# Stick-breaking attention: masks by GpSimd instead of matmuls, and softplus summed over later blocks before the sums' matmuls

## The chip, the cores and the metric

The kernel runs on one core of one Trainium2 chip. The metric is the device time of one execution in microseconds (us). Engines are named as in the profile: PE is TensorE's matmul side, PEld its weight load, DVE is VectorE, ACT is ScalarE, POOL is GpSimd, SP is SyncE, whose queue issues the DMAs.

## The reference

A two-layer decoder trunk over 512 tokens of width 1024: SwiGLU feed-forward, token mixer, feed-forward in each layer. The change is in the mixer of layer 1, stick-breaking attention with 16 heads of 64:

```python
z = jnp.einsum('bhqd,bhkd->bhqk', q_blk, kf) * (dh ** -0.5)
causal = key_pos[None, :] < q_pos[:, None]
log_stay = jnp.where(causal, jax.nn.log_sigmoid(-z), 0.0)
later = lax.cumsum(log_stay, axis=3, reverse=True) - log_stay
a = jnp.where(causal, jnp.exp(jax.nn.log_sigmoid(z) + later), 0.0)
return jnp.einsum('bhqk,bhkd->bhqd', a, vf)
```

With sp = softplus(z), the exponent is z minus the sum of sp over this key and all later ones that the query may see.

## The kernel before, in words

Every matmul operand is split in a high and a low fp32r half, so a product takes two or three matmuls. A head's scores stand with keys on partitions and queries on columns: for key block j (128 keys) only the queries from j*128 on, so the block has `size(j)` = 512 - 128*j columns. They are packed in three PSUM banks (tag `att`, four buffers): bank B holds blocks 1 and 3, bank C block 2, bank A block 0 (`PARTS`).

`stick_scores` (L758) is a head's first half. For each of the banks B, C, A it issues the score matmuls (L765, recorded at L108) and then, on each block's first 128 columns, a mask matmul that adds -1e30 where the key is not earlier than the query (L767, operands `cmask` and `idr`). Then ACT takes Abs, Exp and Ln (L770, L90), DVE forms softplus as max(z, 0) + ln(1 + exp(-|z|)) in an SBUF tile `t` (L773), and DVE splits it into the halves of `sps` (`split_v`: a cast L215, a subtraction L216).

`stick_weights` (L778) is the second half. For each block it adds, on top of z in PSUM, minus the sum of softplus over the block's own keys (`tri`, a triangle of -1) and over every later block (`nones`, a full matrix of -1), by the table `adds`: block 1 takes `nones` over blocks 3 and 2, block 0 over 3, 2 and 1, each in two halves. ACT then takes Exp into `w`, and `split_v` makes the two halves for `attend`, which multiplies with the values into `po`; ACT L529 copies a half of `po` and DVE L530 adds the two.

`stick` (L801) writes PE's order out by hand: with `order["on"]` every matmul depends on the one issued before it. `Flow` is a generator of projection steps of three 512-column (or six 256-column) matmuls each, which are put between the halves of a head: weights of head h, 2 steps, scores of head h+1, 5 steps, `attend` of head h, 5 steps. A finished projection of q or k is scaled by DVE (L547), split (ACT L476, DVE L477) and moved into place by DMAs (L482). The other engines' orders come from a scheduler, so they change with the program.

Tile slots: `t` 5 (both `t` and `w` use them), `sp` 3, `c2` 3 (bank C's halves), `misc` 1.

Of the kernel before, what the change touches and what calls it, by code (L numbers as in the profile page):

```python
# [16 lines left out]
F32R = mybir.dt.float32r  # L17
AF = mybir.ActivationFunctionType
ALU = mybir.AluOpType

P = 128
SEQ = 512
# [6 lines left out]
NEG = -1.0e30  # L29
# [5 lines left out]
def trunk(ctx: ExitStack, tc: tile.TileContext, a: dict, out: bass.AP):  # L35
    nc = tc.nc
    cpool = ctx.enter_context(tc.tile_pool(name="cpool", bufs=1))
# [19 lines left out]
    def T(shape=(P, SEQ), dt=F32, tag="t"):  # L57
        return tmp.tile(list(shape), dt, tag=tag, name=nm(tag), bufs=TMPS[tag])
# [30 lines left out]
    def func(o, i, f, **kw):  # L89
        r = nc.scalar.activation(out=o, in_=i, func=f, **kw)  # L90
        tc.add_manual_dep(r.ins, act["load"].name, nosync, reason="table set order")
        act["used"].append(r.ins)
        return r
# [13 lines left out]
    def mm(*args, **kw):  # L107
        return ordered(nc.tensor.matmul(*args, **kw))  # L108
# [10 lines left out]
    def const_r(name, cols, tag=None):  # L119
        t = cpool.tile([P, cols], F32R, tag=tag or name, name=name)  # L120
        raw = T((P, cols))
        nc.sync.dma_start(raw, a[name])
        nc.vector.tensor_copy(t, raw)
        return t
# [88 lines left out]
    def split_v(hi, lo, src):  # L213

        nc.vector.tensor_copy(out=hi, in_=src)  # L215
        nc.vector.tensor_tensor(out=lo, in0=src, in1=f32(hi), op=ALU.subtract)  # L216
# [246 lines left out]
    def hl(b, tag):  # L463

        return T((P, 2, 256), F32R, "c2") if b[0] == "C" else B((P, 2, SEQ), F32R, tag)
# [289 lines left out]
        return ss  # L755


    def stick_scores(e, q, k, cm, idr):  # L758
        zs, sps = {}, {}
        for b in heads(e):  # L760
            wd = WIDTH[b]
            z = zs[b] = ATT()
            for i, (_, j, at) in enumerate(PARTS[b]):
                scores(z[:, at:at + size(j)], q, k, e, slice(j * P, SEQ), slice(j * P, j * P + P), True,
                       first=i == 0, last=False)  # L765
            for i, (_, j, at) in enumerate(PARTS[b]):
                mm(z[:, at:at + P], idr, cm, start=False, stop=i == len(PARTS[b]) - 1, skip_group_check=True)  # L767
            zw = z[:, :wd]
            t = T()[:, :wd]
            nc.scalar.activation(out=t, in_=zw, func=AF.Abs)  # L770
            func(t, t, AF.Exp, scale=-1.0)
            func(t, t, AF.Ln, bias=one)
            nc.vector.scalar_tensor_tensor(out=t, in0=zw, scalar=0.0, in1=t, op0=ALU.max, op1=ALU.add)  # L773
            sps[b] = hl(b, "sp")
            split_v(sps[b][:, 0, :wd], sps[b][:, 1, :wd], t)
        return zs, sps

    def stick_weights(e, zs, sps, tri, nones):  # L778
        bb, bc, ba = heads(e)

        adds = {2: [(nones, bb, 3 * P, P), (tri, bc, 0, 2 * P)],
                3: [(tri, bb, 3 * P, P)],
                1: [(nones, bb, 3 * P, P), (nones, bc, 0, 2 * P), (tri, bb, 0, 3 * P)],
                0: [(nones, bb, 3 * P, P), (nones, bc, 0, 2 * P), (nones, bb, 0, 3 * P), (tri, ba, 0, SEQ)]}
        banks = {}
        for b in (bc, bb, ba):
            wd = WIDTH[b]
            z = zs[b]
            for _, j, at in PARTS[b]:
                n = size(j)  # L790
                for i, (st, sb, s0, m) in enumerate(adds[j]):
                    for c in range(2):
                        mm(z[:, at + n - m:at + n], st, sps[sb][:, c, s0:s0 + m], start=False,
                           stop=i == len(adds[j]) - 1 and c == 1, skip_group_check=True)
            w = T()[:, :wd]
            func(w, z[:, :wd], AF.Exp)
            banks[b] = hl(b, "ah")
            split_v(banks[b][:, 0, :wd], banks[b][:, 1, :wd], w)
        return banks

    def stick(ss, gcol_next):  # L801
        order["on"] = True
        q0, k0 = ACC(), ACC()
        proj_tile(("sb_q", 0), q0)
        r = norm_r(ss)
        proj_tile(("sb_k", 0), k0)
        rtm = token_r(r)
        r8 = T(tag="r2")
        nc.scalar.mul(out=r8, in_=r, mul=0.125)
        act_set(LNEXP)  # L810
        tri = const_r("tri", P, "bd")
        nones = const_r("nones", P)
        idr = cpool.tile([P, P], F32R, tag="idr", name="idr")
        nc.vector.tensor_copy(idr, ident)
        cm = const_r("cmask", P)
        outs, vs = [], [[] for _ in range(4)]
        q, k = [], []
        plain(q0, r8, lambda y: pack_q(y, "misc"), q)
        plain(k0, r, lambda y: pack_k(y, "misc"), k)

        def stream():
            yield from values(("sb_v", 0), rtm, vs[0])
            for i in range(1, 8):
                yield from plain_steps(("sb_q", i), r8, lambda y: pack_q(y, "misc"), q)
                yield from plain_steps(("sb_k", i), r, lambda y: pack_k(y, "misc"), k)
                if i in (2, 4, 6):
                    yield from values(("sb_v", i // 2), rtm, vs[i // 2])
            yield from out_first("sb_oa", outs)

        flow = Flow(stream())  # L830
        flow.run(16)
        z, o = None, None
        z = stick_scores(0, q[0], k[0], cm, idr)
        flow.run(12)
        for h in range(16):
            p, e = h // 2, h % 2
            banks = stick_weights(e, *z, tri, nones)
            flow.run(2)
            if h < 15:
                n = (h + 1) // 2  # L840
                flow.until(k, n + 1)
                z = stick_scores((h + 1) % 2, q[n], k[n], cm, idr)
            flow.run(5)
            flow.until(vs[p // 2], NB)
            if e == 0:
                o = T(tag="oo")
            attend(vs[p // 2], p, e, banks, o)
            if e == 1:
                out_pair(o, outs)
            flow.run(5)  # L850
        for _ in flow.steps:
            pass
        ss = out_second("sb_ob", outs, gcol_next)
        order["on"] = False
        return ss
# [13 lines left out]
    ident = cpool.tile([P, P], F32, tag="ident", name="ident")  # L869
# [39 lines left out]
def _constants():  # L909
    f = np.float32  # L910
    i = np.arange(P)
    c = {}
    c["ones_ms"] = np.full((P, P), 1.0 / D, f)
    c["bd"] = ((i[:, None] // DH == i[None, :] // DH) / DH).astype(f)
    c["ident"] = np.eye(P, dtype=f)
    c["tri"] = np.where(i[:, None] >= i[None, :], f(-1), f(0)).astype(f)
    c["nones"] = np.full((P, P), -1, f)
    c["cmask"] = np.where(i[:, None] < i[None, :], f(0), f(NEG)).astype(f)

    t = np.arange(SEQ, dtype=f)  # L920

    def angles(half, theta):
        inv = f(1.0) / (f(theta) ** (np.arange(half, dtype=f) / f(half)))
        return t[None, :] * inv[:, None].astype(f)

    ang = angles(32, 10000.0)
    cos, sin = np.cos(ang), np.sin(ang)
    rows_c, rows_s = np.zeros((P, SEQ), f), np.zeros((P, SEQ), f)
    for p in range(P):
        g, j = (p % DH) // 32, p % 32  # L930
        rows_c[p] = cos[g * 16 + j % 16]
        rows_s[p] = sin[g * 16 + j % 16] * (-1 if j < 16 else 1)
    lg = np.log1p(-(2.0 ** (-5.0 - np.arange(8))))
    for n, sign, scale in (("rot_q", 1, 1.0), ("rot_k", -1, DH ** -0.5)):
        dec = scale * np.exp(sign * lg[:, None] * np.arange(SEQ)[None, :])
        dec = np.repeat(dec.reshape(4, 2, SEQ), DH, 1)
        c[n] = np.concatenate([rows_c * dec, rows_s * dec], 2).astype(f)
    ang = angles(8, 500000.0)
    cos, sin = np.cos(ang), np.sin(ang)
    rows_c, rows_s = np.ones((P, SEQ), f), np.zeros((P, SEQ), f)  # L940
    for p in range(P):
        j = p % DH
        if j < 16:
            rows_c[p] = cos[j % 8]
            rows_s[p] = sin[j % 8] * (-1 if j < 8 else 1)
    c["rot_dil"] = np.concatenate([rows_c, rows_s], 1)

    dist = i[:, None] + (SEQ - P) - np.arange(SEQ)[None, :]
    mult = ((dist <= 128).astype(int) + (dist % 4 == 0) * (dist <= 512) + (dist % 16 == 0) * (dist <= 2048)) * (dist >= 0)
    c["dmask"] = np.where(mult > 0, -np.log(np.maximum(mult, 1)), -NEG).astype(f)  # L950
    return {k: np.ascontiguousarray(v, dtype=f) for k, v in c.items()}
# [77 lines left out]
```

## Time and profile before

| | |
|---|---|
| device time, 3 runs | 1997.2, 1992.52, 1995.03; median 1995.03 us |
| profiled execution | 1992.68 us, of which the span from first to last instruction is 1990.9 us |
| granted PE clock, mean | 0.998 |
| busy share of the span | PE 99%, PEld 84%, DVE 54%, ACT 39%, POOL 1% |
| stick-breaking heads | first score matmul at 1370.32 us, last weights' matmuls at 1594 us; a head takes about 14 us |

In a timeline row, the first number is the start in us from the span's start, the second the time until the end of the row's last instruction; then engine, source line, operation, written tile<-read tiles, shape, number of instructions, and in brackets how long the engine was idle before and on whom it waited. A matmul's length includes its way through the array, so what one costs is read from start to start of neighbouring rows.

### The profile page before, as it was taken

The page shows a single profiled execution, that of the slowest core. Times are in us where ns is not written, and L with a number is a line of the kernel's source. Part 1 is how long each engine was busy: PE and PEld are TensorE (multiplying, and loading weights), DVE is VectorE, ACT ScalarE, POOL GpSimd, SP SyncE. Part 2 cuts the span into 40 slices and gives each one's busy share as a digit, 9 for nine tenths or more (in the row PEclk, how much of TensorE's full clock was granted, in tenths as well). Part 3 has the DMA queues.
Part 4 walks back from the last instruction along what each step waited for, and adds up shares of the span by engine and source line. Part 5 has one row for each costly group of instructions (what it writes and reads, how often), then busy time and mean ns, then how long its engine had stood idle before and what let it go on. Part 6 is the DMA issues. An engine that isn't in the chain of part 4 may idle for free.

```text
span 1990.9 us, 24343 instructions
## 1 busy us (share of the span) xinstructions
PE 1972.2 (99%) x9496; PEld 1663.5 (84%) x9496; DVE 1067.3 (54%) x1525; ACT 769.2 (39%) x1140; POOL 18.3 (1%) x40
## 2 busy tenths in 40 slices
PE   8999999999999999999999999999999999999998
PEld 6888888888888888888888888888999888888887
DVE  7665544257867555533455554324676764444334
ACT  5433433223675343322333333223555542222323
POOL 0000000001000000000000000000000000000000
PEclk9999999999999999999999999999999999999999
DMA  7877665687533667633356553336444432223333
GB/s 254 295 264 246 233 199 202 250 258 234 159 104 113 238 235 247 231 97 98 103 202 211 188 201 116 94 129 205 150 152 148 128 134 95 96 101 97 89 97 119
DMA packets 103106, 339.13 MB, mean 170 GB/s; under 512 B 12624, under 2 KB 13392, under 8 KB 99664
## 3 DMA queue, kind: packets, MB, share of 16 engines
q1 hardware_dynamic: 102992, 337.59, 51.3%
q8 instruction: 74, 1.21, 0.2%
q14 instruction: 40, 0.33, 0.0%
HBM read 249.46 MB, written 67.11 MB: 159 GB/s over the span
## 4 chain that ended last, share of the span: by engine, by line
PE 67%; DMA 1%; DVE 0%; ACT 0%; SPq 0%; issue 0%; DVEq 0%; ACTq 0%
PE acc L108 43%; PE att L108 22%; PE po L108 1%; DMA qlo<-misc 0%; DMA t<-tri 0%; DMA qk<-misc 0%; SPq L482 0%; DVE c L352 0%; DVE misc L477 0%; ACT h L238 0%; DVE tp L352 0%; ACT t L246 0%; ACT whl L141 0%; ACT t L90 0%; DVE tp L547 0%
## 5 line engine op out<-in xcount | busy, mean ns | idle before, releaser
L141 ACT CAST whl<-wraw 128x1024 fp32r<-128x1024 f32 (+3 forms) x352 | 355.1, 1010 | 862.4 <-PE acc L108 482.7
L108 PE MATMUL acc<-h,whl 128*128 128x512 f32 x2544 | 604.5, 391 | 6.6 <-ACT h L238 6.1
L108 PEld LDWEIGHTS acc<-h,whl 128*128 128x128 f32 x2544 | 477.0, 188 | 108.7 <-ACT h L238 6.1
L142 DVE TENSOR_TENSOR whl<-wraw,whl 128x1024 fp32r<-128x1024 f32 (+3 forms) x352 | 411.6, 1173 | 279.0 <-ACT whl L141 278.3
L108 PE MATMUL att<-h,whl 128*128 128x512 f32 x2112 | 495.3, 390 | 0.0
L108 PEld LDWEIGHTS att<-h,whl 128*128 128x128 f32 x2112 | 396.5, 188 | 83.6 <-issue 1.2
L108 PE MATMUL acc<-o,whl 128*128 128x512 f32 (+1 forms) x996 | 225.4, 380 | 0.0
L108 PEld LDWEIGHTS acc<-o,whl 128*128 128x128 f32 x996 | 180.3, 188 | 35.0
L401 DVE TENSOR_TENSOR tp<-acc,r 128x512 f32<-128x512 f32 x88 | 60.9, 692 | 179.7 <-PE acc L108 179.5
L407 DVE TENSOR_TENSOR tp<-att,r 128x512 f32<-128x512 f32 x88 | 60.8, 691 | 170.9 <-PE att L108 170.8
L108 PE MATMUL acc<-h,wcut 128*128 128x512 f32 x432 | 105.1, 392 | 0.0
L108 PEld LDWEIGHTS acc<-h,wcut 128*128 128x128 f32 x432 | 79.8, 188 | 16.3
L108 PE MATMUL acc<-v,whl 128*128 128x512 f32 (+1 forms) x408 | 92.9, 377 | 0.0
L108 PE MATMUL acc<-qk,whl 128*128 128x512 f32 (+1 forms) x408 | 92.9, 377 | 0.0
L108 PEld LDWEIGHTS acc<-qk,whl 128*128 128x128 f32 x408 | 73.7, 188 | 14.1
L108 PEld LDWEIGHTS acc<-v,whl 128*128 128x128 f32 x408 | 73.6, 188 | 14.0
L108 PE MATMUL acc<-sp,whl 128*128 128x512 f32 (+1 forms) x306 | 71.0, 377 | 0.0
L108 PE MATMUL acc<-ah,whl 128*128 128x512 f32 (+1 forms) x306 | 71.0, 377 | 0.0
L298 DVE SCALAR_TENSOR_TENSOR x<-acc,x 128x512 f32<-128x512 f32 (+1 forms) x34 | 22.4, 660 | 87.7 <-PE acc L108 87.7
L108 PEld LDWEIGHTS acc<-ah,whl 128*128 128x128 f32 x306 | 55.3, 188 | 10.5
L108 PEld LDWEIGHTS acc<-sp,whl 128*128 128x128 f32 x306 | 55.3, 188 | 10.5
L408 DVE TENSOR_TENSOR tp<-tp,t 128x512 f32<-128x512 f32 x88 | 60.8, 691 | 4.6
(151 smaller groups left out, 1666.9 us busy)
## 6 DMA issues: line engine op xcount, KB each, us to landing
wraw<-f_in SPq DMA_DIRECT2D x174, 512.0 KB, 3.5
wraw<-f_out SPq DMA_DIRECT2D x68, 448.0 KB, 3.3
wraw<-f_out SPq DMA_DIRECT2D x34, 512.0 KB, 3.5
cut_sb_q<-whl SPq DMA_DIRECT2D x16, 512.0 KB, 3.3
cut_sb_k<-whl SPq DMA_DIRECT2D x16, 512.0 KB, 3.4
cut_sb_v<-whl SPq DMA_DIRECT2D x16, 512.0 KB, 3.6
wcut<-cut_sb_q SPq DMA_DIRECT2D x16, 512.0 KB, 4.3
whl<-cut_sb_k SPq DMA_DIRECT2D x8, 1024.0 KB, 5.3
```

The lines of the kernel that those rows point to most:

```text
L108: return ordered(nc.tensor.matmul(*args, **kw))
L141: nc.scalar.copy(out=hi[:, :cols], in_=raw[:, :cols])
L142: lo_eng[0].tensor_tensor(out=lo[:, :cols], in0=raw[:, :cols], in1=f32(hi[:, :cols]), op=ALU.subtract)
L298: nc.vector.scalar_tensor_tensor(out=x[d][:, sl], in0=ps[:, sl], scalar=0.5, in1=x[d][:, sl], op0=ALU.mult, op1=ALU.add)
L401: nc.vector.tensor_mul(out=t1, in0=pg, in1=rr)
L407: nc.vector.tensor_mul(out=t2, in0=pu, in1=rr)
L408: nc.vector.tensor_mul(out=t2, in0=t2, in1=s)
```

## The change

The mask matmuls, `cmask` and `idr` go. `earlier_only` lets GpSimd zero the masked triangle of each block by an affine select, once in the softplus tile `t` before its split, once in the weights `w` after Exp. In `stick_scores` two sums over later blocks are formed on DVE in the same tiles: block 2's softplus plus block 3's (`sps[2]`), and block 1's columns plus those of that sum (`sps[1]`), each split by ACT (high) and DVE (low). Block 1 then takes `nones` over one sum instead of two tiles, block 0 over one instead of three. Of the projection steps, 19 instead of 16 stand ahead of the first head's scores, and 10 instead of 12 between them and its weights.

```diff
+    def earlier_only(t, e, b):
+        for _, _, at in PARTS[b]:
+            nc.gpsimd.affine_select(out=t[:, at:at + P], in_=t[:, at:at + P], pattern=[[1, P]], compare_op=ALU.is_gt,
+                                    fill=0.0, base=0, channel_multiplier=-1)
 ...
-            for i, (_, j, at) in enumerate(PARTS[b]):
-                mm(z[:, at:at + P], idr, cm, start=False, stop=i == len(PARTS[b]) - 1, skip_group_check=True)
 ...
             nc.vector.scalar_tensor_tensor(out=t, in0=zw, scalar=0.0, in1=t, op0=ALU.max, op1=ALU.add)
+            earlier_only(t, e, b)
             sps[b] = hl(b, "sp")
             split_v(sps[b][:, 0, :wd], sps[b][:, 1, :wd], t)
+        bb, bc, _ = heads(e)
+        t1, t2 = ts[bb], ts[bc]
+        nc.vector.tensor_tensor(out=t2[:, P:], in0=t2[:, P:], in1=t1[:, 3 * P:], op=ALU.add)
+        sps[2] = hl(bc, "sp")
+        split(sps[2][:, 0, :], sps[2][:, 1, :], t2)
+        nc.vector.tensor_tensor(out=t1[:, P:3 * P], in0=t1[:, P:3 * P], in1=t2, op=ALU.add)
+        sps[1] = hl(bb, "sp")
+        split(sps[1][:, 0, :3 * P], sps[1][:, 1, :3 * P], t1[:, :3 * P])
 ...
-                1: [(nones, bb, 3 * P, P), (nones, bc, 0, 2 * P), (tri, bb, 0, 3 * P)],
-                0: [(nones, bb, 3 * P, P), (nones, bc, 0, 2 * P), (nones, bb, 0, 3 * P), (tri, ba, 0, SEQ)]}
+                1: [(nones, 2, 0, 2 * P), (tri, bb, 0, 3 * P)],
+                0: [(nones, 1, 0, 3 * P), (tri, ba, 0, SEQ)]}
 ...
             func(w, z[:, :wd], AF.Exp)
+            earlier_only(w, e, b)
             banks[b] = hl(b, "ah")
 ...
-        flow.run(16)
+        flow.run(19)
-        flow.run(12)
+        flow.run(10)
```

**The first place is PE's queue at the weights of head 5**, the head on which the prediction's walk is made. Before (`sp_10979` and `c_1600_10991` are the halves of banks B and C, `sp_11003` of bank A):

```order
L108 MATMUL att_10982<-sp_10979,nones 128x128 x2
L108 MATMUL att_10982<-c_1600_10991,tri 128x256 x2
L108 MATMUL att_10967<-sp_10979,nones 128x128 x2
L108 MATMUL att_10967<-c_1600_10991,nones 128x256 x2
L108 MATMUL att_10967<-sp_10979,tri 128x384 x2
L108 MATMUL att_10967<-sp_10979,tri 128x128 x2
L108 MATMUL att_10994<-sp_10979,nones 128x128 x2
L108 MATMUL att_10994<-c_1600_10991,nones 128x256 x2
L108 MATMUL att_10994<-sp_10979,nones 128x384 x2
L108 MATMUL att_10994<-sp_11003,tri 128x512 x2
```

Now (`c_1613_11034` is `sps[2]`, `sp_11038` is `sps[1]`, `acc_11108` the projection after the one that ends at `acc_11054`):

```order
L108 MATMUL acc_11054<-h_89,wcut_11056 128x512
L108 MATMUL acc_11108<-h_82,whl_11109 128x512 x3
L108 MATMUL att_11009<-sp_11006,nones 128x128 x2
L108 MATMUL att_11009<-c_1609_11018,tri 128x256 x2
L108 MATMUL att_10994<-c_1613_11034,nones 128x256 x2
L108 MATMUL att_10994<-sp_11006,tri 128x384 x2
L108 MATMUL att_10994<-sp_11006,tri 128x128 x2
L108 MATMUL att_11021<-sp_11038,nones 128x384 x2
L108 MATMUL att_11021<-sp_11030,tri 128x512 x2
```

Three pairs of `nones` matmuls are gone, two of 128 columns and one of 256; the two sums are read third and sixth, and the projection step ahead of the weights has become one later.

**The second place is DVE's queue of the same head**, from its first softplus on. Before (`t_10974`, `t_10986`, `t_10998` are softplus of banks B, C, A; `tp` and `misc` belong to a projection, `oo` to the head before):

```order
L773 SCALAR_TENSOR_TENSOR t_10974<-att_10967,t_10974 128x512
L547 TENSOR_TENSOR tp_11012<-acc_10911,r_10022 128x512
L215 CAST sp_10979<-t_10974 128x512
L773 SCALAR_TENSOR_TENSOR t_10986<-att_10982,t_10986 128x256
L216 TENSOR_TENSOR sp_10979<-t_10974,sp_10979 128x512
L477 SCALAR_TENSOR_TENSOR misc_11014<-tp_11012,misc_11014 128x512
L215 CAST c_1600_10991<-t_10986 128x256
L773 SCALAR_TENSOR_TENSOR t_10998<-att_10994,t_10998 128x512
L216 TENSOR_TENSOR c_1600_10991<-t_10986,c_1600_10991 128x256
L215 CAST sp_11003<-t_10998 128x512
L530 TENSOR_TENSOR oo_11036<-po_11037,t_11046 64x512
L216 TENSOR_TENSOR sp_11003<-t_10998,sp_11003 128x512
```

Now, from the softplus of bank A on (`t_11024`; ahead of it stand, as before, those of B and C, each followed by the POOL selects for which its cast waits):

```order
L778 SCALAR_TENSOR_TENSOR t_11024<-att_11021,t_11024 128x512
L216 TENSOR_TENSOR c_1609_11018<-t_11012,c_1609_11018 128x256
L215 CAST sp_11030<-t_11024 128x512
L784 TENSOR_TENSOR t_11012<-t_11012,t_10999 128x128
L216 TENSOR_TENSOR sp_11030<-t_11024,sp_11030 128x512
L211 TENSOR_TENSOR c_1613_11034<-t_11012,c_1613_11034 128x256
L787 TENSOR_TENSOR t_10999<-t_10999,t_11012 128x256
L530 TENSOR_TENSOR oo_11071<-po_11072,t_11081 64x512
L547 TENSOR_TENSOR tp_11096<-acc_11054,r_1454_10057 128x512
L211 TENSOR_TENSOR sp_11038<-t_10999,sp_11038 128x384
```

Behind bank A's split now stand four more DVE operations for the sums, and the last of them, the low half of `sps[1]`, is queued behind L530 and L547.

## Rows read from the trace of the kernel before

**Rows 1.** The page: its heading, the busy times of part 1, and the engines of the chain of waits of part 4.

```profile
span 1990.9 us, 24343 instructions
...
PE 1972.2 (99%) x9496; PEld 1663.5 (84%) x9496; DVE 1067.3 (54%) x1525; ACT 769.2 (39%) x1140; POOL 18.3 (1%) x40
...
PE 67%; DMA 1%; DVE 0%; ACT 0%; SPq 0%; issue 0%; DVEq 0%; ACTq 0%
```

**Rows 2.** All mask matmuls, grouped by tile: count, and ns of one (least, median, most).

```profile
L108 PE MATMUL att<-cmask,idr x64: 220/248/278, 1370.9 to 1583.3; 128*128 128x128 f32 x64
```

**Rows 3.** PE's timeline at the scores of head 5.

```profile
1440.89 0.34 PE L108 MATMUL att<-qk,qk 128*128 128x384 f32 x1
...
1441.41 0.39 PE L108 MATMUL att<-cmask,idr 128*128 128x128 f32 x2
1441.63 0.33 PE L108 MATMUL att<-qk,qk 128*128 128x256 f32 x1
...
1441.92 0.22 PE L108 MATMUL att<-cmask,idr 128*128 128x128 f32 x1
1441.98 0.44 PE L108 MATMUL att<-qk,qk 128*128 128x512 f32 x1
1442.26 0.39 PE L108 MATMUL att<-qlo,qk 128*128 128x512 f32 x1
1442.49 0.22 PE L108 MATMUL att<-cmask,idr 128*128 128x128 f32 x1
```

**Rows 4.** PE's timeline at the weights of head 5.

```profile
1450.71 0.33 PE L108 MATMUL att<-sp,nones 128*128 128x128 f32 x2
...
1451.17 0.34 PE L108 MATMUL att<-sp,nones 128*128 128x128 f32 x2
1451.35 0.45 PE L108 MATMUL att<-c,nones 128*128 128x256 f32 x2
1451.63 0.69 PE L108 MATMUL att<-sp,tri 128*128 128x384 f32 x4
1452.15 0.39 PE L108 MATMUL att<-sp,nones 128*128 128x128 f32 x2
1452.38 0.45 PE L108 MATMUL att<-c,nones 128*128 128x256 f32 x2
1452.66 0.51 PE L108 MATMUL att<-sp,nones 128*128 128x384 f32 x2
1453.01 0.63 PE L108 MATMUL att<-sp,tri 128*128 128x512 f32 x2
```

**Rows 5.** The timeline of DVE (and two rows of ACT) between the scores and the weights of head 5.

```profile
1444.17 0.69 DVE L773 SCALAR_TENSOR_TENSOR t<-att,t 128x512 f32<-128x512 f32 x1 [2.68 <-PE acc L108]
...
1445.38 0.42 DVE L215 CAST sp<-t 128x512 fp32r<-128x512 f32 x1
...
1445.71 0.42 DVE L773 SCALAR_TENSOR_TENSOR t<-att,t 128x256 f32<-128x256 f32 x1
...
1446.05 0.68 DVE L216 TENSOR_TENSOR sp<-t,sp 128x512 fp32r<-128x512 f32 x1
1446.12 0.71 ACT L90 ACTIVATE t<-t,one 128x512 f32<-128x512 f32 x1
...
1447.24 0.29 DVE L215 CAST c<-t 128x256 fp32r<-128x256 f32 x1
1447.43 0.58 ACT L529 COPY t<-po 64x512 f32<-64x512 f32 x1 [0.61 <-PE po L108]
1447.45 0.69 DVE L773 SCALAR_TENSOR_TENSOR t<-att,t 128x512 f32<-128x512 f32 x1
...
1448.71 0.68 DVE L530 TENSOR_TENSOR oo<-po,t 64x512 f32<-64x512 f32 x1
...
1449.31 0.68 DVE L216 TENSOR_TENSOR sp<-t,sp 128x512 fp32r<-128x512 f32 x1
```

**Rows 6.** The timeline of DVE and POOL in two places of layer 0's mixer, where GpSimd already masks the retention scores by affine selects of 256 elements a partition.

```profile
432.28 0.77 POOL L603 TENSOR_SCALAR_AFFINE_SELECT sp<-sp 128x256 fp32r<-128x256 f32 x2 [18.40 <-DVE sp L211]
...
455.84 0.41 POOL L603 TENSOR_SCALAR_AFFINE_SELECT c<-c 128x256 fp32r<-128x256 f32 x1
455.90 0.89 DVE L258 TENSOR_TENSOR t<-t,t 128x512 f32<-128x512 f32 x1
456.19 0.86 POOL L603 TENSOR_SCALAR_AFFINE_SELECT sp<-sp 128x256 fp32r<-128x256 f32 x1
456.82 0.78 DVE L259 SCALAR_TENSOR_TENSOR t<-t,t 128x512 f32<-128x512 f32 x1
```

**Rows 7.** Busy time of the engines in two stretches, with counts: all heads from the first weights to the last, and from the weights of head 4 to those of head 5; then the granted clock, the DMA share and GB/s.

```profile
1380.30:1593.50 213.20, 213.20 (x1301) 193.19 (x1300) 146.94 (x293) 117.68 (x229) 0.00 (x0) 1.00 0.48 150
1436.74:1450.71 13.97, 13.97 (x77) 12.25 (x76) 9.37 (x19) 7.12 (x14) 0.00 (x0) 1.00 0.66 216
```

**Rows 8.** PE's timeline at the first head: its first score matmul and its first weights' matmul.

```profile
1370.32 0.41 PE L108 MATMUL att<-qk,qk 128*128 128x384 f32 x1 [1.92 <-DMA qk<-misc]
...
1380.30 0.33 PE L108 MATMUL att<-sp,nones 128*128 128x128 f32 x2
```

**Rows 9.** The end of head 5's weights and the `attend` that reads them.

```profile
1454.77 0.69 DVE L216 TENSOR_TENSOR ah<-t,ah 128x512 fp32r<-128x512 f32 x1
...
1459.99 0.96 PE L108 MATMUL po<-ah,v 128*128 128x512 f32 x4
```

More of the change, by code (lines that the diff above doesn't have):

```diff
@@ L755, in hybrid, with stick_scores @@
         return ss
-    def stick_scores(e, q, k, cm, idr):
-        zs, sps = {}, {}
+    def earlier_only(t, e, b):
+        for _, _, at in PARTS[b]:
+            nc.gpsimd.affine_select(out=t[:, at:at + P], in_=t[:, at:at + P], pattern=[[1, P]], compare_op=ALU.is_gt,
+                                    fill=0.0, base=0, channel_multiplier=-1)
+    def stick_scores(e, q, k):
+        zs, sps, ts = {}, {}, {}
         for b in heads(e):
@@ L765, in stick_scores @@
                        first=i == 0, last=False)
-            for i, (_, j, at) in enumerate(PARTS[b]):
-                mm(z[:, at:at + P], idr, cm, start=False, stop=i == len(PARTS[b]) - 1, skip_group_check=True)
             zw = z[:, :wd]
-            t = T()[:, :wd]
+            t = ts[b] = T()[:, :wd]
             nc.scalar.activation(out=t, in_=zw, func=AF.Abs)
@@ L812, in stick @@
         nones = const_r("nones", P)
-        idr = cpool.tile([P, P], F32R, tag="idr", name="idr")
-        nc.vector.tensor_copy(idr, ident)
-        cm = const_r("cmask", P)
         outs, vs = [], [[] for _ in range(4)]
@@ L830, in stick @@
         flow = Flow(stream())
-        flow.run(16)
+        flow.run(19)
         z, o = None, None
-        z = stick_scores(0, q[0], k[0], cm, idr)
-        flow.run(12)
+        z = stick_scores(0, q[0], k[0])
+        flow.run(10)
         for h in range(16):
@@ L841, in stick @@
                 flow.until(k, n + 1)
-                z = stick_scores((h + 1) % 2, q[n], k[n], cm, idr)
+                z = stick_scores((h + 1) % 2, q[n], k[n])
             flow.run(5)
@@ L917, in _constants @@
     c["nones"] = np.full((P, P), -1, f)
-    c["cmask"] = np.where(i[:, None] < i[None, :], f(0), f(NEG)).astype(f)
     t = np.arange(SEQ, dtype=f)
```

## The prediction

> **What bounds the kernel now.** I read the page first: PE is busy for 99% of the span, and the chain of waits, followed back from the end, is PE at 67% with 1% for DMA and nothing else worth naming [rows 1]. Then the stretch of the change alone: from the first head's weights to the last head's PE is busy for all of 213.20 us at the full clock (granted 1.00, the 2.4 GHz level), DVE for 146.94 and ACT for 117.68 [rows 7]. So a matmul taken out here is time saved, as long as nothing else comes late at PE. PE's order is fixed by hand: when the operand of one matmul is late, every matmul behind it waits too. The question is therefore what each removed matmul costs, and what slack the longer way from scores to weights still has.
>
> **What is removed.** In each head 4 mask matmuls (64 in all [rows 2]) and, in the weights, 6 `nones` matmuls. I read their cost from start to start. Scores: bank B's two masks hold PE from 1441.41 to 1441.63, 0.22; C's mask starts 0.06 before its follower, but this 512-column one then takes 0.28 to the next start where the second takes 0.23, so C's mask costs 0.11; I price A's the same [rows 3]. Together 0.44. Weights: the pair from 1451.17 to 1451.35 (0.18), from 1452.15 (0.23) and from 1452.38 (0.28), together 0.69 [rows 4]. So 1.13 a head, and times 16 heads **18.1 us**. A removed matmul thus costs 0.11 whether it has 128 or 256 columns.
>
> The Trainium skill ("TensorE: Matmul & The Clock Gate", Back-to-back issue gap) gives 56 ns for an isolated 128-column matmul and about 81 ns in a stream with weight loads; by the smaller figure the sum would be about 11 us, an estimate from that page, and the 0.22 for two masks speaks for neither.
>
> **What is added, on the path.** The low half of `sps[1]` comes last. I walk head 5, t = 0 at its first score matmul, 1440.89 [rows 3]. Its weights began at 9.82 [rows 4]; without the masks at 9.38. Ahead of the second matmul on `sps[1]` stand 0.46 (1450.71 to 1451.17), 0.28, 0.52 and half of 0.35 [rows 4]: it is **needed at 10.81**.
>
> DVE's queue, with starts from start to start [rows 5]: 0.60 for a 512-column operation, 0.34 for 256, casts 0.33 and 0.21. B's softplus began at 3.28 [rows 5]; with B's masks gone it begins at 3.06 and ends at 3.75. Then the selects. None of 128 elements is in the trace; those of 256 take 0.41 alone and 0.36 more for a second one [rows 6]. A select of half the elements lies between 0.18 and 0.41; I take 0.27, near the middle, and 0.20 for the second of a pair. For a step between engines I take 0.05, an estimate. Two selects let B's cast start at 4.32. L477, now queued ahead of it, fills the time before: it waits for ACT's L476, one pass of about 0.6 that starts when B's Ln lets B's softplus begin, so it runs from about 3.7 to 4.3. Softplus of C 4.65; B's low half 4.99; C's cast 5.59 (its select was done at 5.44); softplus of A 5.80, ending 6.49 (its Ln ended at 1446.83, or 5.94, before [rows 5] and ends 0.22 earlier); C's low half 6.40; A's cast 6.86, behind its select; the first sum 7.19 (0.20); A's low half 7.39; low half of `sps[2]` 7.99; second sum 8.33; L530 8.67; L547 9.27; low half of `sps[1]` at 9.87. This is 384 columns, between 0.42 and 0.68 [rows 5]; 0.55 gives 10.42, and 10.47 at PE. That is **0.34 early**. ACT's copies for the high halves (under 0.58 each [rows 5]) run beside DVE's next operations.
>
> **Collisions eat that slack.** In layer 0 the addition L258, which reads two SBUF tiles and starts 0.06 after a select, takes 0.89 where a 512-column addition takes 0.68; the select issued behind it takes 0.86 instead of 0.41 and ends 0.26 after the addition [rows 5, 6]. So the two engines hold each other up. Here the second B select meets L477 (+0.40), C's meets B's low half (+0.25) and A's meets C's low half (+0.2). That is 0.85 at most, a stall of 0.5; none is the other end. I take 0.35. It hits the heads whose queue has both L530 and L547 ahead of the last low half; in the other half L547 stands elsewhere, 0.60 earlier. So 8 x 0.35 = **2.8 us lost**, between 0 and 16 x 0.5 = 8.
>
> The Trainium skill ("SBUF — State Buffer", Who interferes with whom) says that a DVE operation with two SBUF inputs and a reading GpSimd operation share a port pair, held by the first until it ends. The trace agrees (0.89 and 0.86); without that rule the walk would have no loss.
>
> **First head.** PE waited 1.92 there for the moved k [rows 8]. Three more steps of three 0.23-long matmuls, 2.07, now stand ahead of the scores and cover that. But between scores and weights 9.98 [rows 8] become 9.98 - 2 x 0.69 - 0.44 = 8.16, so `sps[1]` is needed at 9.59; the walk's 10.47 to 11.3 gives a stall of 0.9 to 1.7. Net +0.6. The moved steps' weights were issued long before; at the end one step fewer is left, which only moves.
>
> **At nothing.** The selects on `w`: the last low half of the weights ends at 1455.46 and `attend` starts at 1459.99 [rows 9], 4.5 us later; three groups of selects cost at most 2.0, and without that cover they would cost this. The exponent's PSUM banks are freed by Exp, ahead of the selects. `sps` now uses all three `sp` slots, but the slot's last readers are matmuls that stand ahead of the next head's scores. The loads and casts of `cmask` and `idr` lie off PE's path.
>
> **Sum**: 18.1 - 2.8 + 0.6 = 15.9. Against the profiled 1992.68 us this is 1976.8; the median of the runs is 2.35 higher, so **1979 us**.
>
> **Rivals.**
> 1. *Nothing stalls.* For: 0.34 of slack without collisions. Against: collisions are in the trace. 18.1 + 1.9 - 0.9 = 19.1, 1976 us.
> 2. *A short matmul costs only its columns.* For: C's mask starts 0.06 before its follower [rows 3]. Then the eight of 128 and two of 256 columns give 16 x (8 x 0.06 + 2 x 0.12) = 11.5, less 2.2: 9.3, 1986 us. Against: two masks take 0.22. This is what the isolated figure of the Trainium skill's TensorE page (Back-to-back issue gap) would make of it.
> 3. *Every head stalls by about 1 us*, because selects take 0.41 and all collide: the walk grows by 4 x 0.14 + 0.85, so 1.1 late; 18.7 - 16 x 1.1 = 1, 1994 us: no change.
> 4. *DVE becomes the bound: slower.* A head has 13.97 us, and by this sum 12.8 after. DVE's work is 146.94/213.20 of it, 9.6 [rows 7]; the sums add 0.20 + 0.34 + 0.34 + 0.5 = 1.4. Each select group makes DVE wait in its queue, six groups a head. If every wait is bare, with 0.41 per select and 0.10 for the steps, C and A cost 0.5 each and B 0.9, twice: 3.8. Then a head takes 14.9, 0.9 more than before, 16 x 0.9 = 15: 2010 us. It decides from waits of 3.0 a head on; against it, DVE has other work to fill most waits, as in the walk.
>
> **How the numbers follow.** A measurement of this kernel tells some 0.2%, 4 us, from no change. Forecast (13 to 18 gained) 0.55, rival 1 0.12, rival 2 0.11, rival 3 0.13, rival 4 0.08; 0.01 is left. Rival 3 lies around the bound: 0.06 of it faster, 0.07 same. Faster 0.84, same 0.08, slower 0.08. The range runs from 1974, rival 1 and the spread of the runs, to 1990, rival 2 and the part of rival 3 with 0.8 us a stall; rival 4 and the rest of rival 3, some 0.17, are left out.
>
> **What would show it.** After: 9336 matmuls; from weights to weights 12.8 to 13.2 us a head; PE idle ahead of the matmuls on `sps[1]` (waiting for DVE L211), under 0.6 and in every second head; no 1.92 wait at the first scores, but about 1.3 at the first weights; selects near 0.27, some at 0.7 to 0.9. I am wrong if PE waits in every head, if the weights' exponentials become late at `attend`, or if start to start changes where the masks stood by other than 0.11 each.

## The result, and the profile after

The changed kernel takes 1979.69 us (median of 4 runs, 1979.48 to 1980.4) where the kernel before took 1994.33 (4 runs on the same chip, 1992.52 to 1997.2): a ratio of 0.9925, 95% interval 0.9913 to 0.9938, faster by 0.75%. The forecast was 1979.0 within 1974 to 1990. The profiled execution took 1980.4 us.

The page of the changed kernel, and the waits of PE from 1355 to 1600 us (us in all, times, longest):

```profile
span 1978.7 us, 24363 instructions
...
PE 1958.4 (99%) x9336; PEld 1645.7 (83%) x9336; DVE 1089.6 (55%) x1587; ACT 782.4 (40%) x1172; POOL 64.2 (3%) x168
```

```profile
PE att L108 <- DVE sp L211: 2.1, 6, 0.4
PE att L108 <- ACT c L210: 0.5, 1, 0.5
PE att L108 <- issue: 0.4, 1, 0.4
```

160 matmuls are gone [rows 1]. PE now has what it had nowhere in the heads before: it waits for the low half of `sps[1]` (DVE L211). The scores and the weights of head 5 on PE:

```profile
1438.46 0.33 PE L108 MATMUL att<-qk,qk 128*128 128x384 f32 x1
...
1447.87 0.33 PE L108 MATMUL att<-sp,nones 128*128 128x128 f32 x2
...
1448.33 0.40 PE L108 MATMUL att<-c,nones 128*128 128x256 f32 x2
...
1449.09 0.38 PE L108 MATMUL att<-sp,nones 128*128 128x384 f32 x1
1449.82 0.44 PE L108 MATMUL att<-sp,nones 128*128 128x384 f32 x1 [0.34 <-DVE sp L211]
1450.10 0.63 PE L108 MATMUL att<-sp,tri 128*128 128x512 f32 x2
1450.56 0.62 PE L108 MATMUL acc<-h,whl 128*128 128x512 f32 x2
```

The weights last from 1447.87 to the projection's matmul at 1450.56: 2.69, where a head that does not wait takes 2.08 (head 7) and a head before took 2.77. I call the excess over 2.08 a head's **stall**; here it is 0.61. The bracket shows 0.34 of it, since a matmul still in the array counts as busy, so stalls are taken from starts. DVE and POOL in the same head:

```profile
1441.52 0.69 DVE L778 SCALAR_TENSOR_TENSOR t<-att,t 128x512 f32<-128x512 f32 x1 [0.20 <-ACT t L90]
1442.12 0.68 DVE L477 SCALAR_TENSOR_TENSOR misc<-tp,misc 128x512 fp32r<-128x512 f32 x1
1442.28 0.92 POOL L761 TENSOR_SCALAR_AFFINE_SELECT t<-t 128x128 f32<-128x128 f32 x2 [3.69 <-DVE t L778]
1443.24 0.43 DVE L215 CAST sp<-t 128x512 fp32r<-128x512 f32 x1 [0.43 <-POOL t L761]
...
1444.07 0.68 POOL L761 TENSOR_SCALAR_AFFINE_SELECT t<-t 128x128 f32<-128x128 f32 x1 [0.86 <-DVE t L778]
1444.78 0.29 DVE L215 CAST c<-t 128x256 fp32r<-128x256 f32 x1 [0.18 <-POOL t L761]
...
1445.80 0.35 POOL L761 TENSOR_SCALAR_AFFINE_SELECT t<-t 128x128 f32<-128x128 f32 x1 [1.06 <-DVE t L778]
1446.19 0.43 DVE L215 CAST sp<-t 128x512 fp32r<-128x512 f32 x1 [0.18 <-POOL t L761]
...
1448.02 0.68 DVE L530 TENSOR_TENSOR oo<-po,t 64x512 f32<-64x512 f32 x1
1448.62 0.67 DVE L547 TENSOR_TENSOR tp<-acc,r 128x512 f32<-128x512 f32 x1
1449.22 0.54 DVE L211 TENSOR_TENSOR sp<-t,sp 128x384 fp32r<-128x384 f32 x1
```

Each of DVE's three casts waits for its select. The pair of selects on bank B, beside L477, takes 0.92; C's, beside B's low half, 0.68; A's 0.35. Behind them L530 and L547 stand ahead of the last low half, which ends at 1449.76, and PE goes on at 1449.82. The first head:

```profile
1371.42 0.41 PE L108 MATMUL att<-qk,qk 128*128 128x384 f32 x1 [0.36 <-issue]
...
1379.56 0.33 PE L108 MATMUL att<-sp,nones 128*128 128x128 f32 x2
...
1380.66 0.85 PE L108 MATMUL att<-c,nones 128*128 128x256 f32 x2 [0.48 <-ACT c L210]
...
1383.47 0.85 PE L108 MATMUL acc<-h,whl 128*128 128x512 f32 x3
```

The wait of 1.92 for k [rows 8] has become 0.36; the stall at the weights is 3.91 - 2.08 = 1.83. **The account**: heads without a stall follow each other in 12.87 us instead of 13.97 [rows 7], so 16 x 1.10 = 17.6 removed; the first wait gives 1.92 - 0.36 = 1.56; the first head's stall takes 1.83, the others' 5.0. Sum 12.3, and the spans differ by 1990.9 - 1978.7 = 12.2.

### The profile page after: what moved, and what is told of

Read it like the earlier page. It is cut to its first block, busy times and chain, and to the rows that moved or that the text cites. A ratio compares the mean times of both kernels' runs of the same rounds, so it can differ in the third digit from the quotient of the medians.

```text
span 1978.7 us, 24363 instructions
## 1 busy us (share of the span) xinstructions
PE 1958.4 (99%) x9336; PEld 1645.7 (83%) x9336; DVE 1089.6 (55%) x1587; ACT 782.4 (40%) x1172; POOL 64.2 (3%) x168
## 4 chain that ended last, share of the span: by engine, by line
PE 62%; DVE 3%; ACT 1%; POOL 1%; issue 1%; DVEq 0%; ACTq 0%; POOLq 0%
PE acc L108 41%; PE att L108 21%; ACT t L90 1%; POOL t L761 1%; DVE t L778 1%; PE po L108 1%; DVE sp L215 0%; DVE sp L216 0%; ACT t L775 0%; DVE oo L530 0%; DVE sp L211 0%; DVE tp L547 0%; DVE c L211 0%; DVE t L787 0%; DVE c L216 0%
## 5 line engine op out<-in xcount | busy, mean ns | idle before, releaser
L761 POOL TENSOR_SCALAR_AFFINE_SELECT t<-t 128x128 f32<-128x128 f32 x128 | 45.9, 379 | 1036.6 <-DVE t L778 969.0
```

Source lines behind the costliest of these rows:

```text
L761: nc.gpsimd.affine_select(out=t[:, at:at + P], in_=t[:, at:at + P], pattern=[[1, P]], compare_op=ALU.is_gt, fill=0.0, base=0, channel_mult ...
```

## The experiments

Waits and stalls are in us, from starts in each trace; "others" is the sum over heads 1 to 15. A median is that of 4 executions (9 of e8), a ratio is against the kernel before, run beside them (its medians 1994.9 to 1995.1 us, 1994.33 beside the change), and the span is that of the profiled execution alone. The profiled one of e9, 1978.52 us, was its slowest by 1.8 us, so its rows may show more waiting than its median holds.

| run | first scores | head 0 | others | span | median | ratio, 95% interval |
|---|---|---|---|---|---|---|
| the change | 0.36 | 1.83 | 5.0 | 1978.7 | 1979.69 | 0.9925 (0.9913 to 0.9938) |
| e1 masks only | 0 | 0 | 0 | 1982.3 | 1984.0 | 0.9947 (0.9932 to 0.9962) |
| e2 sums only | 0.20 | 0.70 | 0.0 | 1979.5 | 1981.13 | 0.9932 (0.9917 to 0.9947) |
| e6 no selects | 0 | 1.00 | 0.0 | 1972.7 | 1974.7 | 0.99 (0.9886 to 0.9915) |
| e7 selects for nobody | 0 | 1.10 | 0.4 | 1973.3 | 1975.17 | 0.9901 (0.9886 to 0.9915) |
| e8 every select twice | 0 | 1.96 | 14.2 | 1987.0 | 1989.09 | 0.9972 (0.9962 to 0.9982) |
| e5 sums ahead, steps 19, 10 | 0.05 | 1.03 | 0.6 | 1973.0 | 1974.43 | 0.9899 (0.9882 to 0.9915) |
| e9 the same, 19, 12 | 0 | 0 | 5.2 | 1976.8 | 1976.65 | 0.991 (0.9895 to 0.9925) |
| e12 the same, 19, 11 | 0.12 | 0.27 | 4.3 | 1976.0 | 1977.67 | 0.9913 (0.9897 to 0.9928) |
| e14 the same, 16, 12 | 2.11 | 0 | 0.1 | 1973.3 | 1975.89 | 0.9906 (0.9888 to 0.9923) |
| e3 the change, steps 16, 12 | 2.82 | 0 | 1.4 | 1977.1 | 1978.11 | 0.9913 (0.9896 to 0.9929) |
| e10 the change, steps 19, 9 | 0 | 3.09 | 1.3 | 1976.3 | 1977.64 | 0.9912 (0.9894 to 0.993) |

**The two parts, each alone.** e1 keeps the selects and the moved steps, and adds up by matmuls as before:

```diff
-        bb, bc, _ = heads(e)
-        t1, t2 = ts[bb], ts[bc]
 ...
-                1: [(nones, 2, 0, 2 * P), (tri, bb, 0, 3 * P)],
-                0: [(nones, 1, 0, 3 * P), (tri, ba, 0, SEQ)]}
+                1: [(nones, bb, 3 * P, P), (nones, bc, 0, 2 * P), (tri, bb, 0, 3 * P)],
+                0: [(nones, bb, 3 * P, P), (nones, bc, 0, 2 * P), (nones, bb, 0, 3 * P), (tri, ba, 0, SEQ)]}
```

> The change's selects and moved steps, without its sums: the mask matmuls are gone, the nones matmuls stand as before. My theory (a removed mask costs PE 0.10 to 0.11, and the stalls of 0.4 to 0.66 a head come from the sums standing late in VectorE's queue): no stall on later blocks' sums, weights of 2.77 us, a head of about 13.55 instead of 13.97, so 16 x 0.42 + about 1 at the first head = 7 to 8 under the kernel before, ratio 0.996. Rival, the selects by themselves are too late: stalls of about 0.4 in most heads stay and the gain is 1 to 3. Rival, a mask costs only its 128 columns (0.06): gain 4 to 5.

A head takes 13.56, so the masks were worth 0.41 a head, and no head waits. 16 x 0.41 + 1.92 = 8.5; the spans differ by 8.6. The selects alone make nothing late. e2 keeps the sums and the moved steps, and masks by matmuls:

```diff
-            earlier_only(t, e, b)
 ...
+            for i, (_, j, at) in enumerate(PARTS[b]):
+                mm(z[:, at:at + P], idr, cm, start=False, stop=i == len(PARTS[b]) - 1, skip_group_check=True)
 ...
-            earlier_only(w, e, b)
```

> The sums on VectorE and the moved steps, but the masks by matmuls and no select at all. My theory (collisions and waits with GpSimd eat the slack): weights of 2.08 us without the 0.3 to 0.4 wait for the low half of the second sum, at most 0.1 a head; 16 x 0.69 = 11 and about 1 at the first head, so 11 to 12 under the kernel before, ratio 0.994. Rival, the queue's order alone (L530 and L547 ahead of the last low half) makes the stall, GpSimd or not: 0.4 to 0.6 a head stay in the same heads, gain 6 to 7.

The weights take 2.08 and a head 13.29, 0.69 less than before; only the first head stalls. So 0.41 + 0.69 = 1.10 is removed, and neither part alone makes heads 1 to 15 stall. But e2 does not decide between its theory and its rival. The scheduler gave DVE another order there (in head 5 the last low half stands ahead of L530 and L547), and the masks on PE leave each head 0.41 more time. The next two runs decide it.

**What about GpSimd makes them late: the result, or the work beside DVE?** e6 leaves the masking of the diagonal blocks out; in e7 the selects read `t` and `w` and write a tile that nobody reads, so that they still work beside DVE but nobody waits for them (e6's edit, then e7's):

```diff
-            earlier_only(t, e, b)
 ...
-            earlier_only(w, e, b)
```

```diff
-            earlier_only(t, e, b)
+            detached(t, b)
 ...
-            earlier_only(w, e, b)
+            detached(w, b)
 ...
+        for _, _, at in PARTS[b]:
+            nc.gpsimd.affine_select(out=junk, in_=t[:, at:at + P], pattern=[[1, P]], compare_op=ALU.is_gt,
+                                    fill=0.0, base=0, channel_multiplier=-1)
```

> The change without any select: nothing is zeroed, so the masking of the diagonal blocks is left out; everything else stands. My theory: VectorE's casts no longer wait for GpSimd and nothing collides, the last low half comes 0.6 to 0.9 earlier, the stalls of heads 1 to 15 go (5.0 us) and that of the first head halves: 1973.5 to 1975. Rival, the order of VectorE's queue alone: the stalls stay, 1979.

> The change with each select reading the same columns at the same point but writing into a tile that nobody reads: the masking is left out, GpSimd works beside VectorE as in the change, and no cast waits for it. My theory (GpSimd loses the collisions, VectorE only pays by waiting for the late result): selects still take 0.6 to 0.9 in places, VectorE's own operations keep their lengths, no stall in heads 1 to 15, 1974 to 1975.5 as without selects. Rival (the collision slows VectorE itself, by up to 0.2 an operation as at L258 before): stalls of 0.2 to 0.5 stay, 1976.5 to 1979.

Without selects heads 1 to 15 do not stall; with selects for nobody they stall by 0.4 in all. In every one of heads 1 to 15 that stalls in the change, DVE's order from the first softplus to the last low half is the same in both runs as in the change. In e6 the end of that way, in head 5, whose weights start at 1444.73:

```profile
1443.96 0.68 DVE L530 TENSOR_TENSOR oo<-po,t 64x512 f32<-64x512 f32 x1
1444.56 0.68 DVE L547 TENSOR_TENSOR tp<-acc,r 128x512 f32<-128x512 f32 x1
1445.16 0.54 DVE L211 TENSOR_TENSOR sp<-t,sp 128x384 fp32r<-128x384 f32 x1
```

L530 and L547 still stand ahead, but the last low half starts 0.43 behind the weights' start and not 1.35. So the queue's order alone does not make these heads late: the selects make `t` late, and the sums make the way from `t` to PE longer. Groups of DVE and POOL instructions from 1385 to 1590 us (busy us, mean ns of one | idle time before), of e6, of e7 and of the change:

```profile
L216 DVE TENSOR_TENSOR sp<-t,sp 128x512 fp32r<-128x512 f32 x30 | 20.5, 683 | 0.0
...
L215 DVE CAST sp<-t 128x512 fp32r<-128x512 f32 x30 | 12.6, 418 | 0.0
...
L215 DVE CAST c<-t 128x256 fp32r<-128x256 f32 x30 | 8.6, 286 | 0.5 <-ACT t L90 0.5
```

```profile
L216 DVE TENSOR_TENSOR sp<-t,sp 128x512 fp32r<-128x512 f32 x30 | 20.3, 678 | 0.0
...
L215 DVE CAST sp<-t 128x512 fp32r<-128x512 f32 x30 | 14.2, 474 | 0.0
...
L215 DVE CAST c<-t 128x256 fp32r<-128x256 f32 x30 | 11.2, 374 | 0.2 <-ACT t L90 0.2
...
L769 POOL TENSOR_SCALAR_AFFINE_SELECT junk<-t 128x128 f32<-128x128 f32 x120 | 54.6, 455 | 140.8 <-DVE t L786 75.9 <-ACT t L90 60.1
```

```profile
L215 DVE CAST ah<-t 128x512 fp32r<-128x512 f32 x31 | 13.5, 437 | 2.2 <-POOL t L761 2.2
L215 DVE CAST sp<-t 128x512 fp32r<-128x512 f32 x30 | 13.4, 447 | 7.0 <-POOL t L761 7.0
...
L215 DVE CAST c<-t 128x256 fp32r<-128x256 f32 x30 | 9.1, 303 | 3.4 <-POOL t L761 3.4
...
L761 POOL TENSOR_SCALAR_AFFINE_SELECT t<-t 128x128 f32<-128x128 f32 x120 | 43.4, 382 | 156.2 <-DVE t L778 92.7 <-ACT t L90 59.8 <-DVE sp L211 3.1
```

Running beside DVE costs DVE a little (a cast of 512 columns 418 ns without selects, 474 with), its subtractions L216 nothing (683 and 678), and the span 0.6 us at most (1972.7 to 1973.3; the executions of the two runs overlap). What costs 1978.7 - 1973.3 = 5.4 us is that DVE, and behind it PE, waits for the selects' result: 12.6 us of DVE idle in the change's rows, of which 2.2 are at the weights' casts (`ah`) and delay nothing that PE waits for. e8 doubles the selects (each call of `earlier_only` stands twice):

```diff
             earlier_only(t, e, b)
+            earlier_only(t, e, b)
 ...
             earlier_only(w, e, b)
+            earlier_only(w, e, b)
```

> The change with every select issued twice. A select alone is 0.29, so the pair costs another 0.25 or so behind the first, and a second chance to be held up by VectorE. My theory: the last low half comes 0.25 (C), 0.25 (A) and 0.5 (B) later, in all 1.0, so heads with a stall go from 0.6 to 1.3 to 1.6 and those without get 0.5 to 1.0: 12 to 16 us more, 1992 to 1996, and the gain is gone. Rival (the queue behind the selects sets the end, not the selects): under 5 us more, below 1985.

The stalls grow from 6.8 to 16.2 and PE waits for ACT's and DVE's halves of both sums. The span grows by 8.3 us, the median by 9.4: less than the theory's sum and more than the rival's. Heads 3 and 7 still stall by only 0.05, so the slack of some heads swallows the second selects. Heads 1, 5 and 9 stall by 0.6, no more than in the change: there the scheduler put L530 ahead of bank A's cast, so e8 is not the doubled selects alone. The direction is the theory's, the size is not.

**The place of the sums in DVE's queue.** e5 takes the sums ahead of other work that is ready:

```diff
-        bb, bc, _ = heads(e)
-        t1, t2 = ts[bb], ts[bc]
+        with tc.high_priority(offset=SOON):
+            bb, bc, _ = heads(e)
+            t1, t2 = ts[bb], ts[bc]
 ...
```

> The change with the sums and their splits issued at a higher priority, so that in VectorE's queue the last low half stands ahead of L547. My theory: the low half comes 0.6 earlier, the stalls of 0.6 fall to 0 to 0.1 in most heads; of 5.0 us of stalls in heads 1 to 15 some 4 go: 1975 to 1976. Rival, what is late is the selects' wait and not the queue's place: no more than 1 us, 1978.5 to 1980.

DVE and ACT at the end of head 5 in e5, then PE at its weights:

```profile
1445.34 0.68 DVE L530 TENSOR_TENSOR oo<-po,t 64x512 f32<-64x512 f32 x1
1445.46 0.51 ACT L210 CAST sp<-t 128x384 fp32r<-128x384 f32 x1 [0.83 <-DVE t L788]
1446.00 0.56 DVE L211 TENSOR_TENSOR sp<-t,sp 128x384 fp32r<-128x384 f32 x1
1446.48 0.68 DVE L547 TENSOR_TENSOR tp<-acc,r 128x512 f32<-128x512 f32 x1
```

```profile
1445.17 0.33 PE L108 MATMUL att<-sp,nones 128*128 128x128 f32 x2
...
1446.40 0.66 PE L108 MATMUL att<-sp,nones 128*128 128x384 f32 x2
...
1447.35 1.07 PE L108 MATMUL acc<-h,whl 128*128 128x512 f32 x4
```

The low half now stands ahead of L547, and the weights take 2.18 instead of 2.69. In the even heads the priority does more: there both additions stand ahead of bank A's cast, and so no longer behind its select. The stalls of heads 1 to 15 fall from 5.0 to 0.6, with the selects as they are. At 1974.43 us e5 has the lowest median of all runs here, 5.3 us below the change.

**The steps.** e3 is the change with `flow.run(16)` and `flow.run(12)` as before:

```diff
-        flow.run(19)
+        flow.run(16)
 ...
-        flow.run(10)
+        flow.run(12)
```

> The change with the projection steps where they were: 16 ahead of the first scores, 12 behind. My theory: the wait of 1.9 for the moved k returns, the stall of the first weights falls from 1.83 to 0.4; a projection now ends right at the weights of most heads instead of one step earlier, so L547, which stands ahead of the last low half, waits for it: stalls there of 0.6 or more. Together 1979 to 1982. Rival, the position of the projection's end does not matter: the same as the change within 1.

This missed: heads 1 to 15 stall less (0.31 to 0.41 in heads 1, 5, 9 and 13, none elsewhere), not more. The first scores wait 2.82 for k, and this wait costs twice. PE there, and windows of the same stretch (length, busy time and count of PE, PEld, DVE, ACT and POOL, granted clock, DMA share, GB/s):

```profile
1371.62 0.66 PE L108 MATMUL att<-qk,qk 128*128 128x384 f32 x1 [2.82 <-DMA qk<-misc]
...
1373.25 0.63 PE L108 MATMUL att<-qk,qk 128*128 128x512 f32 x1
1373.68 0.63 PE L108 MATMUL att<-qlo,qk 128*128 128x512 f32 x1
1374.11 5.99 PE L108 MATMUL acc<-h,wcut 128*128 128x512 f32 x24
```

```profile
1371.60:1374.10 2.50, 2.48 (x8) 2.32 (x9) 0.00 (x0) 1.14 (x3) 0.00 (x0) 0.50 0.87 299
1374.10:1376.00 1.90, 1.90 (x8) 1.58 (x7) 0.66 (x2) 1.90 (x5) 0.00 (x0) 0.81 0.73 300
1376.00:1379.00 3.00, 3.00 (x14) 2.46 (x14) 2.69 (x8) 1.55 (x3) 0.81 (x4) 1.00 0.09 33
```

Behind the idle stretch the granted clock is 0.50, the 1.2 GHz level, and a 512-column matmul takes 0.43 from start to start instead of 0.23. From the first scores to the first weights e3 needs 11.03; the kernel before needed 9.98 [rows 8], of which 0.41 were masks, so 1.5 are the clock's.

Why do fewer heads stall? e10 has the 28 steps ahead of head 0 that e3 has (the change has 29), but divides them 19 and 9:

```diff
-        flow.run(10)
+        flow.run(9)
```

> The change with 19 steps ahead of the first scores and 9 behind them (28 in all, as in the kernel before and in the run with 16 and 12; the change has 29). Theory: how far the steps' own VectorE rows (L547, L530, L477) lie from the sums decides which heads stall, and that is set by the total of steps ahead of head 0 alone. Then heads 1 to 15 stall as with 16 and 12: 0.3 to 0.4 us in every fourth head, about 1.4 us in all instead of 5.0; the first scores' wait stays at 0.4 us, and the first head, with one step less behind its scores, stalls about 3 us instead of 1.83. Sum about 4.8 instead of 7.2 us of waiting: a profile about 1976.5 us long, median 1976 to 1979. Rival: the stalls come with the fewer steps between the first scores and their weights, whatever the total: then heads 1 to 15 stall as in the change (5.0 us or more), and the time is 1980 us or more.

Heads 1, 5, 9 and 13 stall by 0.30 to 0.32 and no other, as in e3; head 0, one step short, by 3.09. So the total of steps, and not its division, decides which heads stall; the division sets head 0 and the first wait. The traces show by what: with 28 steps both additions stand ahead of bank A's cast in the even heads up to 12, and in heads 1, 5 and 9 L530 has moved ahead of it. e14 puts e3's steps and e5's priority together:

```diff
-        flow.run(19)
+        flow.run(16)
 ...
-        flow.run(10)
+        flow.run(12)
 ...
+        with tc.high_priority(offset=SOON):
```

> The sums of later blocks taken ahead of other VectorE work, with the steps where they were (16 and 12). Theory: with the sums early, the steps' rows can no longer make a head late, so the 0.3 to 0.4 us of every fourth head of the run with 16 and 12 alone go (1.4 us less), and the 2.8 us of the first scores stay: a profile about 1975.7 us long, about 1.3 us more than the 1974.4 us with 19 and 10. Rival: at this total the few stalls left come from something else than the sums' place in VectorE's order, and stay: 1977 to 1978 us.

No head stalls by more than 0.01: 0.1 us in all 16. What is left is the wait of 2.11 for k, behind which the granted clock stayed at 1.00. Its span, 1973.3, is within 0.3 of e5's, but this was its fastest execution: all four of e14 (1975.05 to 1976.75) lie above all four of e5 (1974.28 to 1974.78). Two runs went for e5 without head 0's stall: e9 with `flow.run(12)` and e12 with `flow.run(11)` for `flow.run(10)`.

> The sums at higher priority, and 12 steps instead of 10 between the first head's scores and its weights (19 ahead of the scores as in the change). My theory: the first head's stall of 1.03 goes, since 1.36 more work stands there, and the two steps are missing nowhere later: 1973.4, 1.0 under the same kernel with 10. Rival: the two steps are missing at the end, where the last heads have too few to cover them, and the time stays at 1974.4 or rises.

> The sums of later blocks taken ahead of other VectorE work, with 19 and 11 steps (the run with 10 stalled 1.03 us in the first head and 0.6 in the others; the run with 12 stalled 0 in the first head and 3.13 in the second, where ScalarE's copy L476 waited 2.39 us for a transfer out of misc). Theory: one step more behind the first scores takes the first head's stall away (0 to 0.3 us) and, being a whole step short of the run with 12, does not bring the second head's: 1972.5 to 1974.5 us by the median. Rival: any total other than 29 brings the transfer's wait in, with a stall of 2 us or more in the second head: 1975 to 1977 us.

Both missed. In e9 the second head stalls by 3.13. One row of ACT ahead of it, and PE at the weights:

```profile
1387.18 0.63 ACT L476 ACTIVATE misc<-tp 128x512 fp32r<-128x512 f32 x1 [2.39 <-DMA qlo<-misc]
```

```profile
1392.83 0.33 PE L108 MATMUL att<-sp,nones 128*128 128x128 f32 x2
...
1394.77 0.85 PE L108 MATMUL att<-c,nones 128*128 128x256 f32 x2 [0.92 <-ACT c L210]
```

`misc` has one slot. With two steps more, a projection ends earlier, and ACT's L476 waits 2.39 for the transfers of the one before it, with the head's Ln and Exp queued behind. In e12 that does not happen (head 1 stalls by 0.79), but heads 2, 6 and 10 stall by 0.34 and heads 4, 8 and 12 by 0.66 to 0.67: in head 4 ACT takes another copy (L210 of `o`) between those of the two sums, and DVE's L211 of `o` goes ahead of the last low half. The priority did not pass this work, which was ready before the halves of the sums were.

## Why the prediction was right, and which terms were mis-sized

- **What is removed**: predicted 1.13 a head, measured 1.10. The weights' part is exact (2.77 to 2.08, so 0.69); the masks cost 0.41 (e1), not 0.44, about 0.10 each. 17.6 instead of 18.1. That a removed matmul costs 0.11 "whether it has 128 or 256 columns" does not follow from the prediction's own rows: the two pairs of 128 give 0.09 and 0.12 for each matmul, the pair of 256 gives 0.14, and 0.11 is their average with the masks. Rival 2, a price by columns, is out: 0.10 for 128 columns is nearly twice the 0.06 it needs. The isolated 56 ns of the Trainium skill ("TensorE: Matmul & The Clock Gate", Back-to-back issue gap) does not hold in this stream, and its 81 ns for a stream with weight loads is below the 0.10 to 0.11 measured too.
- **Stalls of heads 1 to 15: mis-sized.** Predicted 8 x 0.35 = 2.8, measured 5.0. The mechanism and the place were right: PE waits for DVE L211 on `sps[1]`, in heads 1, 5 and 9 late by L530 and L547. In head 5 the walk's demand was exact: the second matmul on `sps[1]` would have started 0.17 behind the first, at 1449.27, which is 10.81 after the scores. The operand let it start at 1449.82, or 11.36: 10.47 plus 0.89, all of the 0.85 that the prediction named as its upper end. The selects show it: 0.92 for the pair instead of 0.47, 0.68 for C's instead of 0.27. B's cast starts 0.46 later than in the walk, C's 0.73, A's 0.87, and behind that nothing more is lost. So the lateness should have been 0.5, not 0.35. The condition was wrong too: not every second head stalls but three of four (0.66, 0.38, 0.00, 0.60 in heads 1 to 4). In heads 2 and 4 L547 does stand elsewhere, but with L477 ahead of bank A's softplus, and delays the way there; of the first twelve only heads 3, 7 and 11 have neither.
- **First head: wrong sign, small.** Predicted +0.6, measured 1.56 - 1.83 = -0.3. The last operand came 11.30 after the first score, at the upper end of the walk, and the stall lay above the 0.9 to 1.7 given; without selects (e6) 1.00 of it stays, since two steps fewer stand between scores and weights. Of the first wait 0.36 stayed, put down to issue; in the other runs with 19 steps it is 0 to 0.20.
- **At nothing: held.** The weights' last low half ends 2.6 us ahead of `attend` in head 5 (4.5 before [rows 9]); no PE wait on it appears.
- **Rivals.** 1 (nothing stalls) is what e5 and e14 make true; it gave 1976, and their medians are 1974.43 and 1975.89. 3 would need about 1 us in every head; only e8, with twice the selects, comes near on average. 4 is far: in 207.80 us of heads DVE was busy for 171.44, and its waits for selects are 12.6 in 15 heads, 0.8 each and not 3.0.
- **The number.** By the profile the sum was 3.6 us too hopeful (1976.8 against 1980.4). The median came within 0.7 us since I added the 2.35 by which the profiled execution of before lay under its median, and the one of after lies 0.7 over its own. That nearness is luck; the range is what the terms bear out. The medians differ by 14.6 and the profiled spans by 12.2, and why is open. The executions of the kernel before spread over 4.7 us (1992.5 to 1997.2), those of the change over 0.9. Three traces with 16 steps ahead of the scores waited 1.92, 2.11 and 2.82 for k, and the longest wait cost clock too. If the wait varies so between executions of the kernel before, its median holds more of it than the 1.92 of its profile; no run shows that.

The window that the DVE figures in rival 4 are read from, in the change:

```profile
1382.20:1590.00 207.80, 205.17 (x1172) 181.10 (x1173) 171.44 (x359) 130.85 (x260) 44.18 (x123) 1.00 0.49 154
```

## What to carry to other kernels

When work is taken off a saturated engine and given to others, price what is removed from start to start, and then walk the longer way to the first consumer, in the order of the queues, with the collisions at their upper end. A step that comes last on that way should stand ahead of unrelated work in its queue: issuing the sums and their splits ahead gave back 5.3 us by the medians, as much as leaving the selects out (5.0). And the phase of background steps is a parameter of its own: one step less than 29 changed the stalls of 15 heads from 5.0 to 1.3 us.

## What the runs showed of the hardware that was not expected

- **A wait of PE can cost more than its length.** Behind e3's wait of 2.82 us the granted clock read 0.50 and then 0.81 until about 1376 us, and the stretch became 1.5 us longer. Behind the waits of 2.11 in e14 and 1.92 in the kernel before it stayed at 1.00 in the profiled executions; two of e14's four executions took 1.6 us more than the others. Stalls in pieces did it too: e10's head 0 (3.09 us in all) came with 0.62 from 1381 to 1383.5 us and 0.69 from there to 1386, and the next head came 0.9 later than the stall explains. The 3.13 of e9's second head came with 0.69 from 1395 to 1398 us and 0.74 from there to 1401, and 0.8 more.
- **A select of 128 columns takes 0.29 us alone** (median 294 ns, up to 740), where one of 256 takes 0.41 [rows 6]: half the columns, 0.7 of the time.
- **In collisions GpSimd mostly loses.** Beside DVE's operations with two SBUF inputs the select's time doubles (0.68 beside B's low half in head 5, 0.29 alone) while DVE's hardly changes (0.68); in e7 the casts, with one input, are the ones that lengthen, by 56 ns of 418 and 88 of 286. It is not a rule: the addition L258 lost 0.21 itself [rows 6].
